# Stacking a stick-breaking head's operands three jobs ahead, and filler that runs on into the second group's values

## The chip, the cores and the metric

The kernel runs on one core of one Trainium2 chip. A core has five engines that work side by side, each through its own queue in order: TensorE (PE in the profile, its weight loads PEld) multiplies matrices, VectorE (DVE) and ScalarE (ACT) work element by element, GpSimd (POOL) does the same from on-chip memory only, and SyncE (SP) issues the DMAs. The metric is the time of one execution on the device in microseconds (us), given as the median of several runs.

## What is computed

One layer of a decoder on 512 tokens of width 2048, in float32, with two groups of attention heads side by side:

```python
h = rmsnorm(x, ln_mix)
sb_q, sb_k, sb_v, sw_q, sw_k, sw_v = split(h @ w_in)       # 16 x 64 (three times), 16 x 64, 4 x 64, 4 x 64
# group A, 16 heads, stick-breaking, strictly causal:
z = (sb_q * 64 ** -0.5) @ sb_k.T
log_beta, log_one_minus = log_sigmoid(z), where(causal, log_sigmoid(-z), 0)
survive = reversed_cumsum(log_one_minus) - log_one_minus
out_a = where(causal, exp(log_beta + survive), 0) @ sb_v
# group B, 16 query heads on 4 key heads: window of 128, ALiBi slopes, learned sinks
out_b = softmax_with_sink(sw_q, sw_k, sw_v)
x = x + concat(rmsnorm(out_a), rmsnorm(out_b)) @ w_out
gate, up = split(rmsnorm(x) @ w_gate_up)
x = x + (silu(gate) * up) @ w_down
return rmsnorm(x)
```

## The kernel before

Every float32 operand of a matmul is split into a high part and a rest in a faster float format, and a product is made of three matmuls (high by high, high by rest, rest by high). So each slab of weights that a DMA brings (`raw`) is split once, by ACT (`whi`, L215) and DVE (`wlo`, L216).

**Filler.** The projections lie in a list, `queue`, of slabs; a slab is a list of steps of three matmuls. `step()` issues the next step, and with a slab's third step it loads the slabs behind and splits the next. `pull(ns, mark)` adds `ns` to a running budget, `carry`, and issues steps until the budget is used up or the slab `mark` is reached; a step takes 648 off the budget, or 324 for a step of the second group's values. A budget that can't be spent stays in `carry` for the next `pull`. `drain(mark)` issues all steps up to a mark without touching the budget. In the part that the change touches the list holds, in this order: for each of eight pairs of stick-breaking heads four slabs of eight steps (`add_qk`; L408, L409, L410), four slabs of eight steps for the second group's keys (up to `sb_mark`), and four slabs of sixteen steps for its values (`add_swv`; L376, L377, L378; up to `swv_end`). A pair's projection collects in two banks of on-chip accumulator memory; the last steps of each half end in `q_evac` (L683) or `k_evac` (L686), which scale it on DVE into the tile `qk`. The next pair uses the same two banks.

**The stick-breaking loop.** A job is one block of one head: block 2 (two short key blocks together), block 1, block 0, so 48 jobs for 16 heads. `sb_begin(h)` drains the projection of head h's pair and stacks its operands: the high part of q twice over each other and its rest likewise (`stack_two`: ACT L692, DVE L693, L694, L695), and the high part of k over its rest (`stack_one`: ACT L701, DVE L702), on 64 rows each, so that two matmuls make the scores. `q1`, `q2` and `ks` have two buffers each. One turn j of the loop takes several jobs a stage further:

- `sb_log` (job j): absolute value, exponential, logarithm on ACT (L859 to L861)
- `sb_qk` (job j + 1): the score matmuls (L846, L847) into a bank `z`
- `sb_sum` (job j - 1): the cumulative sums as matmuls (L904) onto the same bank; `sb_w`: exponential and its high part on ACT (L918, L919)
- `sb_sp` (job j): DVE (L866), high part on ACT (L867); `sb_acc`: running sums on POOL (L884 to L894)
- `sb_av` (job j - 2): the output matmuls (L934) and, after a head's block 0, the sum of two halves on ACT and DVE (L706, L708)
- `sb_wsplit` (job j - 1; DVE L924), `sb_lo` (job j; DVE L872), `sb_mask` (job j + 1; DVE L852)

Three times a turn, between these stages, `pull(SBFILL / 3, sb_mark)` adds filler: 3381 a turn, 5.2 steps. The loop runs two turns past the last job. Behind it `drain(sb_mark)` and a `pull` of 16000 issue what is left up to the last slab of the values.

**What follows.** The sliding-window group uses the same list as filler, with a budget of its own per job; ahead of its first scores (L1061) stands `pull(2600.0)`. Its operands `kst` and `qst` are stacked by the same helpers (L692 to L702) into buffers that held the stick-breaking values, and `swv`, the values' tile, takes the buffer of `kq`, from which `qst` is stacked.

The program is written in one order; a scheduler draws up each engine's own order from it, by readiness as it estimates it and by place in the program, except where an instruction is kept in program order.

Of the kernel before, what the change touches and what calls it, by code (L numbers as in the profile page):

```python
# [37 lines left out]
def tile_hymba(ctx: ExitStack, tc: tile.TileContext, x, ln_mix, w_in, sb_norm, swa_norm,  # L38
# [183 lines left out]
    def step():  # L222

        i, m = pos
        sl = queue[i]
        if m == 0:
            split(i)
            if sl["pre"]:
                sl["pre"]()
        if m == min(2, len(sl["mms"]) - 1):  # L230
            for k in (1, 2):
                if i + k < len(queue):
                    load(i + k)
            if i + 1 < len(queue):
                split(i + 1)
        t = sl["mms"][m](sl["hi"], sl["lo"])
        pos[1] += 1
        if pos[1] == len(sl["mms"]):
            pos[0] += 1
            pos[1] = 0  # L240
            if sl["post"]:
                sl["post"]()
        for d in list(due):
            d[0] -= 1
            if d[0] <= 0:
                due.remove(d)
                d[1]()
        return t

    def pull(ns, mark=None):  # L250

        mark = len(queue) if mark is None else mark
        carry[0] += ns
        while carry[0] > 0 and pos[0] < mark:
            carry[0] -= step()
# [4 lines left out]
    def drain(mark=None):  # L260

        mark = len(queue) if mark is None else mark
        while pos[0] < mark:
            step()
# [423 lines left out]
    def stack_two(src, r0, hi, lo):  # L688

        s64 = src[r0:r0 + HD]  # L690
        r1 = HD - r0
        A.activation(out=hi[r0:r0 + HD], in_=s64, func=AF.Copy)  # L692
        V.tensor_copy(out=hi[r1:r1 + HD], in_=s64)  # L693
        V.tensor_tensor(out=lo[r0:r0 + HD], in0=s64, in1=f(hi)[r0:r0 + HD], op=ALU.subtract)  # L694
        V.tensor_copy(out=lo[r1:r1 + HD], in_=f(lo)[r0:r0 + HD])  # L695

    def stack_one(src, r0, st):

        s64 = src[r0:r0 + HD]
        r1 = HD - r0  # L700
        A.activation(out=st[r0:r0 + HD], in_=s64, func=AF.Copy)  # L701
        V.tensor_tensor(out=st[r1:r1 + HD], in0=s64, in1=f(st)[r0:r0 + HD], op=ALU.subtract)  # L702
# [38 lines left out]
    def sbt(dt, name, n=512, bufs=1):  # L741
        return phase[1].tile([P, n], dt, tag=name, name=name, bufs=bufs)
# [65 lines left out]
    sb_mark = len(queue)  # L808
    add_swv()
    swv_end = len(queue)  # L810
# [10 lines left out]
    def sb_begin(h):  # L821
        drain(marks[h // 2])
        H = Head()
        heads[h] = H
        H.r0 = (h % 2) * HD
        qk = qks[h // 2]
        H.q1, H.q2, H.ks = sbt(F32R, "q1", bufs=2), sbt(F32R, "q2", bufs=2), sbt(F32R, "ks", bufs=2)
        stack_two(qk[:, 0, :], H.r0, H.q1, H.q2)
        stack_one(qk[:, 1, :], H.r0, H.ks)
        H.acc = [None] * 3  # L830
        H.blk = [None] * 3
# [110 lines left out]
    jobs = [(h, i) for h in range(16) for i in (2, 1, 0)]  # L942
    NJ = len(jobs)

    def at(fn, j):
        if 0 <= j < NJ:
            fn(*jobs[j])

    SBFILL = SB_SLABS * 8 * 648.0 / 46
# [2 lines left out]
    at(sb_qk, 0)  # L952
    at(sb_mask, 0)
    for j in range(NJ + 2):
        if j + 2 < NJ and jobs[j + 2][1] == 2:
            sb_begin(jobs[j + 2][0])
        at(sb_log, j)
        at(sb_qk, j + 1)
        pull(SBFILL / 3, sb_mark)
        at(sb_sum, j - 1)  # L960
        at(sb_w, j - 1)
        at(sb_sp, j)
        at(sb_acc, j)
        pull(SBFILL / 3, sb_mark)
        at(sb_av, j - 2)
        at(sb_wsplit, j - 1)
        at(sb_lo, j)
        at(sb_mask, j + 1)
        pull(SBFILL / 3, sb_mark)
    drain(sb_mark)  # L970
    pull(16000.0, swv_end - 1)


    swp = open_phase("swp", 15)
# [161 lines left out]
    jobs = [(g, blk) for g in range(4) for blk in range(NT)]  # L1136
    NJ = len(jobs)
# [715 lines left out]
```

## Time and profile before

| what | us |
|---|---|
| three runs | 2018.45 median, 2017.85 to 2019.76 |
| the profiled execution's own time | 2018.88 |
| its span, from the first instruction to the last | 2017.2 |
| PE busy | 1989.7 |
| ACT busy | 1512.6 |
| DVE busy | 1478.7 |
| POOL busy | 1121.8 |
| score matmuls of the stick-breaking loop, first to last start | 162.6 to 419.9 |

A row of a group names the line, the engine, the operation, out<-in by tile, the shape, the count, the busy time and the mean duration in ns, then the engine's idle time just before and what ended it. A row of waits names who waited, for whom, the total in us, how often, and the longest. A row of the timeline begins with start and duration in us. A busy PE is not PE at its peak, since the ends of matmuls are modelled; between full-rate matmuls of 512 columns the timeline has 0.23 us from start to start.

### The profile page before, as it was taken

The numbers are of one execution on the slowest core, as the hardware profiler recorded it, in microseconds if no ns is written. First come the engines' busy times: TensorE is split into PE (matmuls) and PEld (weight loads), VectorE is DVE, ScalarE is ACT, GpSimd is POOL, SyncE is SP. The second block draws the span as 40 slices with busy tenths as digits, with TensorE's granted clock in tenths as the row PEclk, the third lists the DMA queues.
The fourth block names the chain that finished last, engine by engine and source line by source line (L and its number), as shares of the span: only waits on it lengthen the run. The fifth ranks groups of instructions, "written<-read, shape, count | busy, mean of one in ns | idle before, by whom it ended". The sixth has DMA issues, their size and how long they took to land.

```text
span 2017.2 us, 29170 instructions
## 1 busy us (share of the span) xinstructions
PE 1989.7 (99%) x10268; PEld 1697.7 (84%) x10268; DVE 1478.7 (73%) x1972; ACT 1512.6 (75%) x2031; POOL 1121.8 (56%) x599
## 2 busy tenths in 40 slices
PE   9999999999999999999999999999999999999998
PEld 8888777788888888888888888888888888888886
DVE  6677777767984777777777777777777867767767
ACT  6766777766773478777777777777777788788787
POOL 2833445430010066766667666666766778878883
PEclk9999999999999999999999999999999999999999
DMA  6412222122233354453544535444353643533523
GB/s 205 140 57 80 63 60 62 60 71 74 94 126 121 117 166 119 117 139 101 138 113 123 133 103 142 109 127 130 106 141 106 265 157 111 178 129 107 174 86 115
DMA packets 283298, 240.23 MB, mean 119 GB/s; under 512 B 11024, under 2 KB 233296, under 8 KB 280720
## 3 DMA queue, kind: packets, MB, share of 16 engines
q1 hardware_dynamic: 281392, 231.52, 38.6%
q0 software_dynamic: 1376, 5.52, 0.8%
q8 instruction: 81, 1.33, 0.3%
q10 hardware_dynamic: 384, 1.34, 0.2%
q14 instruction: 65, 0.53, 0.1%
HBM read 218.40 MB, written 19.92 MB: 118 GB/s over the span
## 4 chain that ended last, share of the span: by engine, by line
PE 89%; DVE 5%; ACT 4%; issue 2%; DMA 0%; DVEq 0%; ACTq 0%; POOL 0%; POOLq 0%
PE o L118 36%; PE m L118 30%; PE m L408 2%; PE m L410 2%; PE m L409 2%; PE m L376 2%; PE m L378 1%; PE m L377 1%; PE z L118 1%; PE o L377 1%; PE o L376 1%; PE o L378 1%; PE z L904 1%; DVE l L872 1%; ACT e L918 1%
## 5 line engine op out<-in xcount | busy, mean ns | idle before, releaser
L118 POOL TENSOR_TENSOR t<-raw,t 128x1024 f32<-128x1024 f32 x111 | 282.3, 2543 | 281.3 <-ACT hp L118 263.5
L118 DVE TENSOR_TENSOR wlo<-t,hp 128x1024 fp32r<-128x1024 f32 x247 | 301.2, 1219 | 184.3 <-PE o L118 112.9
L118 ACT ACTIVATE whi<-t 128x1024 fp32r<-128x1024 f32 x247 | 262.2, 1061 | 126.2 <-PE o L118 76.4
L118 POOL TENSOR_TENSOR t<-raw,raw 128x1024 f32<-128x1024 f32 x114 | 295.2, 2593 | 22.4 <-issue 11.3
L118 PE MATMUL o<-hca,whi 128*128 128x512 f32 x880 | 307.5, 391 | 0.0
L118 DVE TENSOR_TENSOR wlo<-raw,hp 128x1024 fp32r<-128x1024 f32 x187 | 228.2, 1221 | 92.1 <-issue 51.7
L118 ACT ACTIVATE whi<-raw 128x1024 fp32r<-128x1024 f32 (+1 forms) x189 | 200.0, 1058 | 105.0 <-PE m L118 74.8
L118 ACT ACTIVATE hp<-t 128x1024 fp32r<-128x1024 f32 x247 | 249.1, 1009 | 2.6 <-POOL t L118 2.6
L118 PE MATMUL o<-hca,wlo 128*128 128x256 f32 x880 | 244.0, 280 | 0.0
L118 ACT ACTIVATE hp<-raw 128x1024 fp32r<-128x1024 f32 x191 | 192.9, 1010 | 3.0 <-DMA raw<-in_w_down_dram 2.0
L118 PEld LDWEIGHTS o<-hca,whi 128*128 128x128 f32 x880 | 164.2, 187 | 35.8
L118 PE MATMUL m<-hca,whi 128*128 128x512 f32 x528 | 186.3, 392 | 1.1 <-DVE hca L118 1.1
L118 PEld LDWEIGHTS o<-hca,wlo 128*128 128x128 f32 x880 | 165.6, 189 | 0.4
L216 DVE TENSOR_TENSOR wlo<-raw,whi 128x1024 fp32r<-128x1024 f32 x87 | 110.4, 1269 | 65.0 <-ACT whi L215 64.5
L215 ACT ACTIVATE whi<-raw 128x1024 fp32r<-128x1024 f32 x87 | 91.8, 1055 | 78.4 <-PE o L378 32.4
L118 PE MATMUL m<-whi,dca 128*128 128x512 f32 x592 | 146.9, 389 | 0.0
L118 PE MATMUL o<-whi,dca 128*128 128x512 f32 x592 | 146.9, 389 | 0.0
L118 PE MATMUL m<-hca,wlo 128*128 128x256 f32 x528 | 146.3, 280 | 0.0
L118 PEld LDWEIGHTS o<-whi,dca 128*128 128x128 f32 x592 | 111.0, 188 | 23.2
L118 PEld LDWEIGHTS m<-whi,dca 128*128 128x128 f32 x592 | 111.0, 188 | 23.0
L408 PE MATMUL m<-hhi,whi 128*128 128x512 f32 x320 | 126.8, 396 | 2.2 <-DVE qk L686 2.1
L118 PE MATMUL m<-hcs,whi 128*128 128x512 f32 x352 | 125.9, 392 | 0.0
(371 smaller groups left out, 5233.6 us busy)
## 6 DMA issues: line engine op xcount, KB each, us to landing
raw<-in_w_gate_up_dram SPq DMA_DIRECT2D x348, 256.0 KB, 5.2
raw<-in_w_down_dram SPq DMA_DIRECT2D x68, 512.0 KB, 4.9
raw<-in_w_in_dram SPq DMA_DIRECT2D x35, 512.0 KB, 3.7
raw<-in_w_in_dram SPq DMA_DIRECT2D x66, 256.0 KB, 3.3
raw<-in_w_out_dram SPq DMA_DIRECT2D x32, 512.0 KB, 3.7
aT<-w SPq DMA_DIRECT2D x44, 256.0 KB, 3.5
xd<-aT SPq DMA_DIRECT2D x10, 1024.0 KB, 7.3
rx<-in_w_down_dram SPq DMA_DIRECT2D x20, 512.0 KB, 5.9
```

The costliest lines, as they stand in the source:

```text
L118: return lambda *a, **k: tc.keep_in_program_order(fn(*a, **k))
L215: A.activation(out=hi, in_=raw, func=AF.Copy)
L216: V.tensor_tensor(out=lo, in0=raw, in1=f(hi), op=ALU.subtract)
L376: mm(o, lhsT=lh[:, sl], rhs=hi[:, j, :], start=first, stop=False, skip_group_check=halves)
L377: mm(o, lhsT=lh[:, sl], rhs=lo[:, j, :], start=False, stop=False, skip_group_check=halves)
L378: mm(o, lhsT=ll[:, sl], rhs=hi[:, j, :], start=False, stop=(k == nslab * a - 1), skip_group_check=halves)
L408: mm(o, lhsT=wh, rhs=xh, start=(k == 0), stop=False)
L409: mm(o, lhsT=wh, rhs=xl, start=False, stop=False)
L410: mm(o, lhsT=wl, rhs=xh, start=False, stop=(k == KT - 1))
L872: V.tensor_tensor(out=B.l[:, a:w], in0=B.e, in1=f(B.h)[:, a:w], op=ALU.subtract)
L904: mm(zb[:, o:o + r.shape[1]], lhsT=lhsT, rhs=r, start=False, stop=last, skip_group_check=True)
L918: A.activation(out=B.e, in_=B.z, func=AF.Exp)
```

## The change

Two things, both in the stick-breaking loop. `sb_begin` of the next head (and in it the drain of that head's pair) is issued three jobs ahead, which is in the turn of the running head's block 2, where it was two jobs ahead, in the turn of block 1. And the three pulls in the loop may run on through the second group's values up to the last of their slabs, where they stopped at `sb_mark`; the pull behind the loop gets a budget of 6000 in place of 16000.

```diff
     for j in range(NJ + 2):
-        if j + 2 < NJ and jobs[j + 2][1] == 2:
-            sb_begin(jobs[j + 2][0])
+        if j + 3 < NJ and jobs[j + 3][1] == 2:
+            sb_begin(jobs[j + 3][0])
         at(sb_log, j)
         at(sb_qk, j + 1)
-        pull(SBFILL / 3, sb_mark)
+        pull(SBFILL / 3, swv_end - 1)
         at(sb_sum, j - 1)
         at(sb_w, j - 1)
         at(sb_sp, j)
         at(sb_acc, j)
-        pull(SBFILL / 3, sb_mark)
+        pull(SBFILL / 3, swv_end - 1)
         at(sb_av, j - 2)
         at(sb_wsplit, j - 1)
         at(sb_lo, j)
         at(sb_mask, j + 1)
-        pull(SBFILL / 3, sb_mark)
+        pull(SBFILL / 3, swv_end - 1)
     drain(sb_mark)
-    pull(16000.0, swv_end - 1)
+    pull(6000.0, swv_end - 1)
```

## The prediction

> **What bounds the kernel now.** I read the page first, then the busy time by stretches, then TensorE's waits in the stretches that are not full, then the timeline around the longest wait.
>
> ```profile
> span 2017.2 us, 29170 instructions
> PE 1989.7 (99%) x10268; PEld 1697.7 (84%) x10268; DVE 1478.7 (73%) x1972; ACT 1512.6 (75%) x2031; POOL 1121.8 (56%) x599
> ```
>
> TensorE (PE) is the bound. No matmul is added or dropped, so the change can move only time in which PE stands still or runs at a lower clock: 2017.2 - 1989.7 = 27.5 us, plus the clock. The stretches say where; the columns are the stretch, its length, then busy time and count of PE, weight loads, VectorE (DVE), ScalarE (ACT) and GpSimd (POOL), the granted clock, the DMA share and GB/s.
>
> ```profile
> 160.00:213.00 53.00, 53.00 (x258) 45.02 (x257) 37.73 (x60) 39.00 (x72) 21.03 (x32) 1.00 0.24 70
> 200.00:240.00 40.00, 37.62 (x173) 31.20 (x173) 29.40 (x45) 30.29 (x56) 18.07 (x24) 0.96 0.21 60
> 320.00:360.00 40.00, 35.81 (x165) 28.41 (x164) 31.20 (x48) 30.43 (x55) 21.03 (x26) 1.00 0.19 53
> 400.00:424.00 24.00, 22.49 (x108) 18.38 (x107) 16.05 (x26) 18.75 (x34) 14.27 (x20) 1.00 0.21 67
> 424.00:452.00 28.00, 26.25 (x203) 24.86 (x202) 20.62 (x31) 17.27 (x29) 6.11 (x7) 1.00 0.24 76
> 730.00:2000.00 1270.00, 1268.60 (x6737) 1094.28 (x6737) 935.25 (x1046) 1013.84 (x1109) 883.92 (x361) 1.00 0.45 130
> ```
>
> From 730 us on PE is full, and the first 53 us of the stick-breaking loop are full too. The holes lie between 213 and 436 us, inside that loop. PE's waits from 200 to 400 us, then from 400 to 445 us (total, times, longest):
>
> ```profile
> PE z L846 <- DVE ks L702: 6.9, 5, 2.2
> PE m L408 <- DVE qk L686: 2.1, 4, 1.6
> PE o L934 <- DVE l L924: 0.5, 2, 0.3
> ...
> PE o L934 <- ACT h L919: 2.3, 2, 1.6
> PE o L934 <- DVE l L924: 1.0, 3, 0.4
> ```
>
> Together 12.8 us. The largest is what the change names: the score matmuls of a new head (L846) wait for the last operand that is stacked (L702). The timeline of the longest, DVE first, then PE:
>
> ```profile
> 215.68 0.42 DVE L693 CAST q<-qk 64x512 fp32r<-64x512 f32 x1
> 217.30 0.56 DVE L866 SCALAR_TENSOR_TENSOR e<-z,e 128x384 f32<-128x384 f32 x1 [1.20 <-ACT e L861]
> 217.77 0.68 DVE L924 TENSOR_TENSOR l<-e,h 128x512 fp32r<-128x512 f32 x1
> 218.37 1.23 DVE L694 TENSOR_TENSOR q<-qk,q 64x512 fp32r<-64x512 f32 x1
> 219.53 0.63 DVE L872 TENSOR_TENSOR l<-e,h 128x384 fp32r<-128x384 f32 x1
> 220.09 0.67 DVE L686 TENSOR_TENSOR qk<-m,rbc 128x512 f32<-128x512 f32 x1
> 220.80 0.67 DVE L695 CAST q<-q 64x512 fp32r<-64x512 f32 x1
> 221.50 1.64 DVE L216 TENSOR_TENSOR wlo<-raw,whi 128x1024 fp32r<-128x1024 f32 x1
> 223.17 0.68 DVE L702 TENSOR_TENSOR ks<-qk,ks 64x512 fp32r<-64x512 f32 x1
> ...
> 220.82 0.50 PE L408 MATMUL m<-hhi,whi 128*128 128x512 f32 x1 [0.17 <-DVE qk L686]
> 221.39 0.40 PE L410 MATMUL m<-hhi,wlo 128*128 128x512 f32 x1
> 224.00 0.35 PE L846 MATMUL z<-q,ks 128*128 128x256 f32 x1 [2.21 <-DVE ks L702]
> ```
>
> DVE works almost without a pause from 217.30 to 223.85: evacuation (L686), stacking (L693 to L695, L702), the running head's chain (L866, L924, L872) and a filler split (L216) share these 6.5 us, and the next head's scores come due in the middle. The wait has an after-effect on the clock:
>
> ```profile
> 220.00:225.00 5.00, 2.62 (x12) 0.99 0.10 30
> 225.00:230.00 5.00, 5.00 (x20) 0.67 0.26 76
> ```
>
> At a granted clock of 0.67 the second stretch loses 5 x 0.33 = 1.65 us, with the first (5 x 0.01) **1.7 us**. The clock is 1.00 in the other stretches shown, so the shorter waits did not do this. The Trainium skill ("TensorE: Matmul & The Clock Gate", Part 1) has the clock fall back only after an idle window of about 3.4 us; the trace does not agree, since 2.21 us preceded a fall here. By the page's rule this term would be nil and the forecast below about 1.7 us later.
>
> **The change, part by part.** One job (one of three blocks of one head) takes 5.5 us: 47 jobs lie between the first and last start of this row.
>
> ```profile
> L846 PE MATMUL z<-q,ks x64: 277/333/393, 162.6 to 419.9; 128*128 128x256 f32 x32, 128*128 128x384 f32 x16, 128*128 128x512 f32 x16
> ```
>
> *Stacking three jobs ahead.* All 15 stackings in the loop, with the drain ahead of each, move up one job, past one round of filler and chain on ACT and DVE; no DMA is issued other than those of the filler steps, in their order on SP. The buffers (two of each operand) are free in time: those of head h - 2 are read last in the score matmuls issued two jobs earlier. The operands gain about 5.5 us on their use, and the longest lateness is 2.2 us. So the five waits go: **-6.9 us**, and with them the clock stretch: **-1.7 us** (bounds 0 and the whole for both).
>
> Every head pair's projection must be drained one job earlier. Counting the steps in the code (648 each against 3381 a job, 5.2 steps), the drain before head 2 grows from 4 steps to 10; the later ones stay at 0 or 1. Ten steps of 0.68 us (three matmuls 0.23 us apart) are work that PE does anyway. What could stop it there is the next slab's split; in 131 to 154 us filler ran alone and PE was full:
>
> ```profile
> 131.00:154.00 23.00, 23.00 (x105) 18.75 (x104) 16.23 (x27) 12.37 (x20) 0.35 (x2) 1.00 0.41 118
> ```
>
> So 0, at worst one late split, 1.6 us (L216 above).
>
> What is late next: the next pair's filler still needs the two banks that L683 and L686 empty. Those 2.1 us stay as they are: 0, between -2.1 (a less crowded job) and +2.1 (as much again).
>
> The stacking now falls into the job that runs block 2, ahead of its L866, L924 and L872 on DVE. Those feed L904 and L934 one and two jobs later. The trace shows what displaced chain steps cost now: 0.5 us in 200 to 400 us. I take 1.0 us more, **+1.0**; the bounds are 0 and 15 stackings at 0.4 us, the longest such wait, 6 us. I stay near the low end because at the old place the crowd is larger: there it also meets the head's output sum (L708, below), and the new job has none.
>
> *Filler into the second group's values.* Before, the projection steps end in job 45 by the same count; jobs 46 to 49 have no filler of their own, and 48 value steps follow behind the loop. Now jobs 45 to 49 take 9, 10, 11, 10 and 8 of them.
>
> ```profile
> L376 PE MATMUL m<-whi,hhi x64: 278/283/386, 423.8 to 452.0; 128*128 128x256 f32 x64
> L376 PE MATMUL m<-whi,hhi x44: 280/283/386, 436.3 to 452.0; 128*128 128x256 f32 x44
> L934 PE MATMUL o<-l,vst x64: 274/337/502, 175.4 to 435.8; 128*128 128x256 f32 x32, 128*128 128x384 f32 x16, 128*128 128x512 f32 x16
> L1061 PE MATMUL z<-kst,qst x64: 277/283/283, 463.9 to 593.3; 128*128 128x256 f32 x64
> L702 DVE TENSOR_TENSOR qst<-kq,qst x8: 676/686/690, 430.3 to 439.1; 64x512 fp32r<-64x512 f32 x8
> L686 DVE TENSOR_TENSOR kq<-m,rbc x2: 674/676/679, 418.9 to 423.3; 128x512 f32<-128x512 f32 x2
> L708 DVE TENSOR_TENSOR oA<-o,oc x3: 683/684/684, 411.8 to 437.8; 64x512 f32<-64x512 f32 x3
> ```
>
> Of 64 value steps (one L376 each, the first row) 44 run after the last output matmul (started at 435.8), only 20 beside the waiting chain; the L934 waits there are 3.3 us. With a full ration each job resembles those of 200 to 400 us. I take **-2.5 us** (0 to -3.3), not all, because the stacking for the second group (L702, 430.3 to 439.1) stays on DVE. A seam is added: the value steps need the banks that L686 empties at 418.9 and 423.3. At 2.1 us over seven such seams that is **+0.3** (0 to 1.6, the longest).
>
> The time behind the loop gets shorter. Now 27.6 us of pure filler lie between the end of the last output matmul (435.8 + 0.5) and the first window scores (463.9). After the change the budget gives 16 value steps (15.7/44 = 0.36 us each) and 7 projection steps (0.68): 10.5 us. The scores need stacks that end by 440 us, 4 us after the last output matmul, so it suffices. Later waits of that phase may shift; the longest I found there in the whole trace is
>
> ```profile
> PE z L1112 <- DVE s L1104: 2.4, 2, 1.5
> ```
>
> so **+0.5** (-2.4 to +1.5).
>
> **Sum**: -6.9 - 1.7 + 1.0 - 2.5 + 0.3 + 0.5 = **-9.3 us**. The profiled execution took 2018.88 us, 1.7 more than its span; 2018.88 - 9.3 = 2009.6. The median shown is 2018.45, 0.4 lower: **2009.2 us**.
>
> **The rivals.** *The wait only moves.* DVE does the same work, and what it does earlier delays something else: the banks (L408) or the outputs (L934) take back the 6.9 us. For it: DVE is busy 29 to 31 of 40 us here. Against: in 160 to 213 us, with the same work per job, DVE was busy 37.7 of 53 us and no wait came up, so a job's delay can be worked off in the next. Then 2018.45 - 1.7 - 2.5 + 0.8 = **2015.0**.
>
> *It doesn't do what it says.* The order on each engine is drawn up from the program by a scheduler; 20 value steps already run ahead of their place in the program. If it puts the stacking where it was, the waits stay: **2018**.
>
> *Slower: the stacking in front of the chain.* A head's four DVE pieces (L693 0.42 and L702 0.68, L694 and L695 at the same, as their shapes are the same: 2.2 us) stand together ahead of L866 and L924. Between the end of L924 (218.45) and its reader L934 (219.36) lie
>
> ```profile
> 219.36 0.39 PE L934 MATMUL o<-h,vst 128*128 128x512 f32 x1
> ```
>
> 0.9 us, so 1.3 us per head, 15 heads, 20 us: 2018.45 - 6.9 - 1.7 - 2.5 + 0.8 + 20 = **2028**. It decides from (6.9 + 1.7 + 2.5 - 0.8)/15 = 0.7 us a head. Against it: these pieces stood in the chain's way in the other job too, where L934 lost 0.5 us in all. The Trainium skill (the same page, on engine queue depths) has ACT and DVE work strictly first in, first out, which is this rival's condition.
>
> *Everything goes*, bank waits and tail included: 2018.45 - 6.9 - 1.7 - 3.3 - 2.1 = **2004.4**.
>
> **How the numbers follow.** Forecast 0.60, wait moves 0.14, no effect 0.10, slower 0.08, everything 0.08. A measurement tells 0.2%, 4 us, from no change: faster means under 2014.4. The forecast (but for 0.02), all of "everything" and 0.05 of "moves" lie there: 0.71. The rest of "moves", the forecast's 0.02 and nearly all of "no effect" make 0.20, the slower rival and 0.01 from "no effect" 0.09. The range of 8 in 10 runs from 2005.0, the forecast without the rest of the tail (0.8), the displaced chain (1.0), the two seams (0.8) and most of the bank waits (1.6), to 2017.0, 2 us past the moved wait; it leaves out the slower rival, most of "no effect" and half of "everything".
>
> **What would show it.** In the profile after, L846 <- L702 should be gone or under 0.5 us, the clock 1.00 from 160 to 440 us, L934's waits behind 400 us under 1 us, and L376 should start about five jobs before the last L934 with about 20 of its steps, not 44, behind it. L408 <- L686 should stand near 2 us. I am wrong if L934 or L904 waits grow past 5 us inside the loop, if L1061's first start waits for a stack, or if the stacking's place on DVE is unchanged.

## The result, and the profile after

The changed kernel takes 2003.18 us (median of four runs, 2002.74 to 2003.48), the kernel before 2018.51 on the same chip: a ratio of 0.9924 with a 95% interval of 0.9912 to 0.9936, 15.3 us less. The forecast was 2009.2 with a range from 2005.0 to 2017.0, so the direction was right and the gain is 6 us larger than forecast, outside the range. The profiled execution of the changed kernel took 2003.03 us, against 2018.88.

From the page after:

```profile
span 2000.9 us, 29118 instructions
PE 1983.5 (99%) x10268; PEld 1697.5 (85%) x10268; DVE 1479.4 (74%) x1972; ACT 1512.2 (76%) x2031; POOL 1115.7 (56%) x599
```

The same counts on the five engines, 16.3 us less span. PE's busy time fell by 6.2 us with the same matmuls; that is the first sign that "busy" had hidden a loss. The stretches, with the columns as before:

```profile
160.00:213.00 53.00, 53.00 (x255) 44.82 (x254) 38.98 (x60) 38.30 (x69) 20.86 (x30) 1.00 0.27 79
200.00:240.00 40.00, 40.00 (x194) 33.95 (x193) 29.67 (x47) 32.20 (x59) 20.98 (x30) 1.00 0.23 67
320.00:360.00 40.00, 39.29 (x193) 33.06 (x192) 32.46 (x51) 32.86 (x61) 18.66 (x26) 1.00 0.20 60
400.00:424.00 24.00, 24.00 (x166) 22.53 (x165) 16.83 (x27) 20.41 (x36) 9.24 (x13) 1.00 0.21 67
424.00:452.00 28.00, 26.41 (x168) 23.97 (x167) 20.36 (x44) 14.65 (x30) 2.40 (x4) 1.00 0.25 76
```

The holes of 200 to 240 and 400 to 424 us are closed, the one of 320 to 360 us has shrunk from 4.2 to 0.7 us, and the granted clock stays at 1.00. PE's waits after, from 200 to 400 us and then from 400 to 445 us:

```profile
PE o L934 <- DVE l L924: 2.6, 4, 1.2
PE m L408 <- DVE qk L683: 0.7, 2, 0.4
...
PE m L376 <- DVE swv L268: 1.6, 1, 1.6
```

L846 no longer waits for a stacking. The waits at the outputs (L934) inside the loop are five times what they were, and there is a new one: the last slab of the value steps waits for the evacuation of its own bank.

Of the signs that the prediction named, one failed plainly: the waits for L686 did not stay near 2 us, they are gone, and 0.7 us for L683 stand there. L376 starts at 408.0 us, four jobs and not five before the last L934, and 17 of its steps lie behind that.

Shown waits fell from 12.8 to 4.9 us, 7.9 us; the span fell by twice that. To find the rest I added up, over the trace's matmuls, the time from one start to the next less 0.2268 us per 512 columns (the pace of the timeline's undisturbed 512-column matmuls). This sum is the **loss**. "Loop" is from the first L846 to the last head's first L846, "tail" on to the last L934, "seam" on to the first window scores (L1061), "window" on to the last matmul of that phase (L1126). In us:

| kernel | loop | tail | seam | window |
|---|---|---|---|---|
| before | 18.7 | 6.0 | 1.2 | 12.7 |
| the change | 8.5 | 1.1 | 2.1 | 10.7 |
| difference | -10.2 | -5.0 | +0.9 | -2.1 |

That is -16.4 us, the span's difference to 0.1. In loop and tail before, 24.7 us were lost where the wait list shows 12.9. Not all of it is waiting: 4.0 us are delays of under 0.02 us each, of which the changed kernel has as many (4.6 us), and 1.6 us are the stretch at half clock. The other 19.1 us stand against the 12.9 shown. One reason can be seen in single rows: a matmul's row is 0.39 us long but the next may start 0.23 after it, so a matmul that is late by up to 0.16 us shows no wait at all, and every shown wait is 0.16 us too short. In the kernel before:

```profile
220.27 0.39 PE L410 MATMUL m<-hhi,wlo 128*128 128x512 f32 x1
```

The next matmul started at 220.82 (in the prediction), 0.55 us later: 0.32 us lost, 0.17 shown.

### The profile page after: what moved, and what is told of

It reads as the page before. It is cut to its first block, busy times and chain, and to the rows that moved or that the text cites. A ratio compares the mean times of both kernels' runs of the same rounds, so it can differ in the third digit from the quotient of the medians.

```text
span 2000.9 us, 29118 instructions
## 1 busy us (share of the span) xinstructions
PE 1983.5 (99%) x10268; PEld 1697.5 (85%) x10268; DVE 1479.4 (74%) x1972; ACT 1512.2 (76%) x2031; POOL 1115.7 (56%) x599
## 4 chain that ended last, share of the span: by engine, by line
PE 93%; DVE 3%; ACT 3%; issue 1%; DVEq 0%; POOL 0%; ACTq 0%; POOLq 0%
PE o L118 36%; PE m L118 30%; PE m L408 3%; PE m L409 3%; PE m L410 2%; PE m L376 2%; PE m L378 2%; PE m L377 2%; PE z L118 1%; PE o L378 1%; PE o L376 1%; PE o L377 1%; PE z L904 1%; PE o L934 1%; PE z L1112 1%
## 5 line engine op out<-in xcount | busy, mean ns | idle before, releaser
L118 POOL TENSOR_TENSOR t<-raw,t 128x1024 f32<-128x1024 f32 x111 | 282.3, 2543 | 281.1 <-ACT hp L118 262.8
L118 POOL TENSOR_TENSOR t<-raw,raw 128x1024 f32<-128x1024 f32 x114 | 294.7, 2588 | 23.5 <-issue 12.1
L216 DVE TENSOR_TENSOR wlo<-raw,whi 128x1024 fp32r<-128x1024 f32 x87 | 108.7, 1249 | 56.0 <-ACT whi L215 53.7
L408 PE MATMUL m<-hhi,whi 128*128 128x512 f32 x320 | 125.9, 393 | 0.7 <-DVE qk L683 0.7
```

The source lines that it names most:

```text
L118: return lambda *a, **k: tc.keep_in_program_order(fn(*a, **k))
L216: V.tensor_tensor(out=lo, in0=raw, in1=f(hi), op=ALU.subtract)
L408: mm(o, lhsT=wh, rhs=xh, start=(k == 0), stop=False)
```

## The experiments

All were timed beside the kernel before on the same chip (2018.1 to 2018.5 us). The loss is from each kernel's profiled execution. Some of these hold stretches of 3.4 us at half clock, up to 1.7 us of loss each: one in the seam of stack1, drain4_fill, sum_later and drain4_sum_later, one in the window phase of stack3_only, drain5_fill and drain5_sum_later, two in that of drain6_fill.

| kernel | us | ratio to before, 95% | loop | tail | seam | window |
|---|---|---|---|---|---|---|
| stack3_only | 2009.13 | 0.9957 (0.9944 to 0.9969) | 8.5 | 4.6 | 1.1 | 14.4 |
| fill_only | 2012.99 | 0.9975 (0.9965 to 0.9985) | 18.6 | 1.5 | 1.9 | 10.6 |
| post6000_only | 2017.22 | 0.9994 (0.9985 to 1.0004) | 18.6 | 6.0 | 1.2 | 11.0 |
| drain3_stack2 | 2007.21 | 0.9951 (0.9938 to 0.9963) | 7.1 | 5.3 | 1.1 | 12.5 |
| drain3_fill | 2003.34 | 0.9920 (0.9908 to 0.9933) | 7.1 | 1.1 | 2.7 | 10.6 |
| stack1 | 2003.78 | 0.9925 (0.9911 to 0.9938) | 7.1 | 1.1 | 4.0 | 10.8 |
| drain4_fill | 2013.44 | 0.9973 (0.9962 to 0.9984) | 16.1 | 3.9 | 1.6 | 11.1 |
| stack4 | 2016.89 | 0.9991 (0.9981 to 1.0000) | 20.0 | 3.9 | 0.3 | 12.4 |
| drain5_fill | 2022.28 | 1.0019 (1.0010 to 1.0028) | 19.9 | 4.7 | 0.1 | 17.4 |
| drain6_fill | 2015.32 | 0.9983 (0.9974 to 0.9992) | 6.5 | 2.5 | 0.1 | 23.5 |
| split5 | 2003.58 | 0.9923 (0.9911 to 0.9936) | 9.1 | 1.1 | 2.1 | 10.6 |
| drain4_split5 | 2013.22 | 0.9973 (0.9963 to 0.9984) | 16.7 | 3.9 | 0.3 | 12.5 |
| sum_later | 2006.68 | 0.9942 (0.9928 to 0.9957) | 10.2 | 1.1 | 4.4 | 10.7 |
| drain5_sum_later | 2021.92 | 1.0019 (1.0009 to 1.0029) | 19.9 | 4.7 | 0.1 | 16.0 |
| drain4_sum_later | 2012.04 | 0.9968 (0.9957 to 0.9980) | 15.5 | 3.9 | 1.8 | 10.9 |

### The two parts of the change, one by one

stack3_only, the kernel before with

```diff
-        if j + 2 < NJ and jobs[j + 2][1] == 2:
-            sb_begin(jobs[j + 2][0])
+        if j + 3 < NJ and jobs[j + 3][1] == 2:
+            sb_begin(jobs[j + 3][0])
```

> The kernel before with the stacking and its drain three jobs ahead, and the pulls as they were. Theory A (the change is two parts that add up; a wait of PE costs what the starts of its matmuls lose, more than the idle time shown): L846 <- L702 is gone (-8.5 us from start to start), the half clock is gone (-1.6), the bank waits L408 <- L686 fall by some 3, L934's waits in the loop grow by about 2.5, and the tail behind 410 us keeps its 3 us of waits: 2018.5 - 10.6 = 2008. Rival B (the gain of 15.3 us is the stacking's alone, the filler part is worth nothing): 2003 to 2004. Rival C (the parts need each other, since both move the same filler): 2014 or more.

fill_only, the kernel before with the other lines:

```diff
-        pull(SBFILL / 3, sb_mark)
+        pull(SBFILL / 3, swv_end - 1)
...
-    pull(16000.0, swv_end - 1)
+    pull(6000.0, swv_end - 1)
```

> The kernel before with the pulls of the change (filler into the values inside the loop, 6000 behind it) and the stacking two jobs ahead. Theory A: the tail's waits go (-4), one wait for the values' evacuation comes (+1.8), the window phase gains 2: 2018.5 - 4.5 = 2014. The five L846 waits and the half clock stay. Rival B: 2018 to 2019. Rival C: 2016 to 2018, with tail waits left over 2 us.

post6000_only, the last line alone:

> The kernel before with only the budget behind the loop cut from 16000 to 6000. By the count of steps the same 48 value steps are issued there (the unspent budget of jobs 46 to 49 is 13000), but 10000 less is carried into the window phase. Theory A: if the window phase's 2 us come from the lower budget, L1112's waits fall from 2.4 to under 0.5 us and the time is 2016 to 2017. Rival: they come from where the values run, and the time is 2018 to 2019 with L1112's waits as before.

The parts gain 9.2 and 5.4 us, 14.6 together, where the change gains 15.3: they add up, each within 1.2 us of theory A, and rivals B and C are out. The loss table says which part acts where: the stacking's part takes the loop from 18.7 to 8.5 us and leaves 4.6 us of the tail; the filler's part leaves the loop at 18.6 and takes the tail to 1.5. In the wait list of fill_only, from 200 to 445 us, the loop's old waits stand all but untouched:

```profile
PE z L846 <- DVE ks L702: 6.9, 5, 2.2
PE m L408 <- DVE qk L686: 1.8, 2, 1.6
PE o L934 <- DVE l L924: 0.6, 2, 0.3
```

The lower budget alone takes the window phase from 12.7 to 11.0 us, with L1112's waits down from 2.4 to 0.2 us as its theory A said. Its time lies 1.1 us lower; that is inside the interval, so of the time alone it can't be told.

post6000_only answers a second question, by chance. Its first long wait is as long as in the kernel before, but no stretch at half clock follows it, and then the next head's wait is there, which the kernel before did not have at that place:

```profile
224.14 0.35 PE L846 MATMUL z<-q,ks 128*128 128x256 f32 x1 [2.22 <-DVE ks L702]
257.33 0.36 PE L846 MATMUL z<-q,ks 128*128 128x256 f32 x1 [1.32 <-DVE ks L702]
```

With the fall of the clock the loop before lost 8.5 us at L846 and L847 and 1.6 in the slow stretch; without it 9.7 and nothing. That fits ACT and DVE catching up during the slow stretch, so that 1.2 of its 1.6 us come back at the next wait; over the whole loop the loss is 18.7 us with the fall and 18.6 without.

### Is it the lead of the stacking?

Three kernels separate the drain of a pair's projection from the stacking. drain3_stack2 is the kernel before with the drain alone three jobs ahead:

```diff
+        if j + 3 < NJ and jobs[j + 3][1] == 2:
+            drain(marks[jobs[j + 3][0] // 2])
         if j + 2 < NJ and jobs[j + 2][1] == 2:
             sb_begin(jobs[j + 2][0])
```

> The kernel before with the drain of a pair's projection three jobs ahead, but the stacking itself left two jobs ahead, pulls as they were. Theory P (what counts is that the projection ends earlier, so that its evacuation and the stacking don't fall into one job): L846 waits under 1 us, bank waits as in stack3_only, time within 1.5 us of it, 2007 to 2009.5. Rival S (what counts is the stacking's own place in the program, which puts its instructions ahead of others on DVE): L846 waits of 4 us and more stay, 2012 or more.

drain3_fill is the same with the filler into the values; stack1 has the stacking one job ahead, in the turn that reads it:

```diff
+        if j + 3 < NJ and jobs[j + 3][1] == 2:
+            drain(marks[jobs[j + 3][0] // 2])
-        if j + 3 < NJ and jobs[j + 3][1] == 2:
-            sb_begin(jobs[j + 3][0])
+        if j + 1 < NJ and jobs[j + 1][1] == 2:
+            sb_begin(jobs[j + 1][0])
```

> The changed kernel with the stacking put back to two jobs ahead, its drain left three ahead (with the filler into the values). Theory A (the loop, the tail and the window phase add up, and the drain's place is what the loop gains by): no L846 wait, loop losses as in drain3_stack2 (1.4 us less than the change), the rest as in the change: 2003.2 - 1.4 = 2001.8, between 2001 and 2003.5. Rival S (the stacking's place in the program matters once the tail is full too): 2005 or more.

> The changed kernel with the drain three jobs ahead, but the stacking one job ahead, in the turn whose score matmuls read it. It measures the price of a wait. Theory A: the L846 waits are back where a stacking isn't ready; with n such waits of W us together by the wait list, the time is that of drain3_fill plus W + 0.2 to 0.25 n (what the overlap of matmul ends hides), whatever the granted clock shows. Rival C (the clock's falls add their own 1.7 us each): time over that sum by 1.7 for each stretch at half clock. If the scheduler starts the stackings early by itself (their inputs are ready), W is under 2 us and the time as drain3_fill.

The stacking's own place in the program shows nothing in the time: with it three, two or one job ahead that is 2003.2, 2003.3 and 2003.8 us. stack1 has no L846 wait at all, so it could not measure the price of one. The traces show why. L686 for the pair of heads 4 and 5 starts at 220.1 us in the kernel before, and at 215.3 to 215.8 in the changed kernel and these three; head 4's last piece of stacking (L702) ends at 223.9 before, and at 218.2 to 219.1 in the four, wherever the program has the stacking. What the line `j + 3` moves is the end of the projection. That agrees with theory P, though drain3_stack2 lies 1.9 us below stack3_only where 1.5 was allowed: with the stacking two or one job ahead the loop loses 7.1 us, not 8.5. The 1.4 us forecast from this for drain3_fill didn't show in the median; 0.6 of them went to its last value slab, which waits 2.2 us in place of 1.6.

### Is it the lead of the drain?

drain4_fill, drain5_fill and drain6_fill have the drain four, five and six jobs ahead and the stacking two; stack4 has both four ahead. The edit of drain5_fill, against drain3_fill:

```diff
-        if j + 3 < NJ and jobs[j + 3][1] == 2:
-            drain(marks[jobs[j + 3][0] // 2])
+        if j + 5 < NJ and jobs[j + 5][1] == 2:
+            drain(marks[jobs[j + 5][0] // 2])
```

> The same with the drain four jobs ahead, in the turn that runs block 0, the stacking two ahead. Theory L (the lead counts: any turn early enough will do): no L846 wait, bank waits L408 of 1 us or less, 2001 to 2004. Rival T (the turn counts: the bank waits fell because the turn of block 2 has no output sum on DVE): bank waits of 2 us and more are back, with the losses they bring 2004 to 2007.

> The changed kernel with drain and stacking four jobs ahead (head 1 is stacked ahead of the loop). Theory A: there is no L846 wait left to win; the time stays within 2 us of the change, 2001.5 to 2005. Rival (the displaced chain, the slower case of the prediction: a stacking further ahead stands in front of more of the running head's work): L934 and L904 waits grow from 2.6 us to over 6, 2007 or more.

> The changed kernel with the drain five jobs ahead, which is the turn of block 1 again, as before the change, the stacking two ahead. Theory T (what costs is the turn in which a pair's projection ends, with the split of the next slabs tied to it; the lead counts only until the stacking is ready): no L846 wait, losses at L408 and L934 in the loop as in the kernel before (5 us from start to start, 1.8 more than drain3_fill), time 2003.5 to 2007. Rival L (the further ahead, the worse: 3 gives 2003.3, 4 gives 2013.4): 2014 or more.

> The same with the drain six jobs ahead, the turn of block 2, as in the change. Theory T: the loop's losses are those of drain3_fill (7 us in all, L934 2.6, L408 0.8); the filler ends 16 steps sooner, so some of the tail's waits come back: 2004 to 2008. Rival L: 2014 or more, with loop losses over 16 us.

No kernel of these has an L846 wait, and yet in two of the three turns the loop loses about as much as before the change (16.1 to 20.0 us against 18.7). Waits from 163 to 400 us in drain5_fill (the turn of block 1, as before the change), drain4_fill (block 0) and drain6_fill (block 2, as in the change):

```profile
PE o L934 <- DVE l L924: 7.4, 16, 1.1
PE m L408 <- DVE qk L683: 1.0, 2, 0.5
PE m L408 <- DVE qk L686: 0.7, 3, 0.4
```

```profile
PE o L934 <- DVE l L924: 5.5, 7, 1.5
PE m L408 <- DVE qk L686: 2.0, 5, 0.6
```

```profile
PE o L934 <- DVE l L924: 1.9, 3, 1.2
```

By turn, the loop's loss is 18.7 and 19.9 us (block 1: two and five ahead), 16.1 and 20.0 (block 0: drain4_fill, stack4), and 8.5, 7.1, 7.1, 7.1 and 6.5 (block 2: three and six ahead). The lead does not order them, the turn does. So theory T held for the loop, and rival L, which expected over 16 us there for six jobs ahead, is out. The times alone would not say so: 2022.3 us for drain5_fill and 2015.3 for drain6_fill both lie where rival L had them. Theory T's price for drain5_fill was too low by a factor of three: it expected 5 us at L408 and L934, and 15.8 were lost there. drain6_fill is slow for a reason of its own: its filler runs out sooner, and the window phase loses 23.5 us, of which the last value slab's wait for L268 alone is 5.2. drain4_fill and stack4 went against their first theories: bank waits of 2.0 us are back in the one, at a time 6 us past what rival T allowed, and L934 and L904 wait 8.4 us in the other.

What a wrong turn does can be read at drain5_fill's longest wait. First ACT, PE and DVE rows of one job, from the end of its sums to its output (other rows left out):

```profile
280.73 0.40 PE L904 MATMUL z<-l,negu 128*128 128x512 f32 x1
280.92 1.05 ACT L215 ACTIVATE whi<-raw 128x1024 fp32r<-128x1024 f32 x1
281.88 0.61 ACT L692 ACTIVATE q<-qk 64x512 fp32r<-64x512 f32 x1
283.42 0.62 ACT L701 ACTIVATE ks<-qk 64x512 fp32r<-64x512 f32 x1
284.46 0.47 ACT L918 ACTIVATE e<-z 128x384 f32<-128x384 f32 x1
285.44 0.51 ACT L919 ACTIVATE h<-e 128x384 fp32r<-128x384 f32 x1
287.40 0.55 DVE L924 TENSOR_TENSOR l<-e,h 128x384 fp32r<-128x384 f32 x1
288.00 0.39 PE L934 MATMUL o<-l,vst 128*128 128x256 f32 x1 [1.10 <-DVE l L924]
```

and what DVE did ahead of that L924:

```profile
284.59 1.11 DVE L694 TENSOR_TENSOR q<-qk,q 64x512 fp32r<-64x512 f32 x1
285.74 0.69 DVE L702 TENSOR_TENSOR ks<-qk,ks 64x512 fp32r<-64x512 f32 x1
286.35 0.41 DVE L695 CAST q<-q 64x512 fp32r<-64x512 f32 x1
286.79 0.69 DVE L866 SCALAR_TENSOR_TENSOR e<-z,e 128x512 f32<-128x512 f32 x1
```

The sums end at 281.1, the exponential (L918) starts 3.3 us later, behind a filler split and two pieces of stacking on ACT; its high part (L919) is done at 285.95, and L924 starts 1.4 us later, behind three pieces of stacking and L866 on DVE. In this job that is the prediction's slower rival, the stacking ahead of the chain, in another turn than the one it was feared for. In the changed kernel a job of block 0 runs like this (other rows left out), with no stacking in its way, and L924 ends 2.5 us before its reader:

```profile
296.94 0.39 PE L904 MATMUL z<-l,negu 128*128 128x512 f32 x1
299.22 0.58 ACT L918 ACTIVATE e<-z 128x512 f32<-128x512 f32 x1
299.83 0.63 ACT L919 ACTIVATE h<-e 128x512 fp32r<-128x512 f32 x1
300.50 0.69 DVE L924 TENSOR_TENSOR l<-e,h 128x512 fp32r<-128x512 f32 x1 [0.54 <-ACT h L919]
303.71 0.39 PE L934 MATMUL o<-l,vst 128*128 128x512 f32 x1
```

Over heads 2 to 13 the mean time from the last L904 of a job to its L918 is 2.7, 2.2 and 1.8 us for blocks 2, 1 and 0 in the changed kernel, and 3.5, 4.3 and 4.0 in drain5_fill.

But most jobs of drain5_fill are late without any stacking in the way. Of these 36 jobs 13 have a piece of it on ACT between their last L904 and L918, and L918 comes 3.5 us after on average; in the other 23 it comes 4.2 us after. What goes with the turn is the order of the jobs on ACT: the chain of the job two later (its L859) runs ahead of a job's L918 in 35 of the 36 in drain5_fill, 31 in the kernel before, 29 in drain4_fill and 28 in stack4, but in 22 in the changed kernel, 21 in drain3_fill and 25 in drain6_fill. L924 is done on average 0.45 us ahead of its output matmul in drain5_fill and 0.75 in drain4_fill, and 1.8, 2.0 and 2.2 us ahead in the last three.

### Why the turn matters: two tries that missed

split5 and drain4_split5 issue the split of the next filler slab later, since the waits that are left had an L216 ahead of L924:

```diff
-        if m == min(2, len(sl["mms"]) - 1):
+        if m == min(5 if 11 <= i < 43 else 2, len(sl["mms"]) - 1):
```

> The changed kernel with the split of the next filler slab (ACT L215, DVE L216) issued with a slab's sixth step instead of its third, for the slabs of the loop. Theory W (the waits L934 <- L924 that are left come from a split of 1.2 us that stands right ahead of L924 on DVE): L934's waits fall from 2.6 us to under 1, 2000.5 to 2002.5. Rival (the split comes late and the filler waits for it): PE waits for whi or wlo of 2 us and more, 2004 or more.

> drain4_fill with the split issued with a slab's sixth step. Theory W: L934's 8 us of waits fall to under 3, the time from 2013.4 to 2009 or less. Rival (they come from the stacking and evacuation in the turn of block 0, not from the split): L934's waits stay over 6 us, 2012 or more.

Theory W fell: the times are the same within the intervals, L934 waits 3.3 us in split5, more than the change's 2.6, and drain4_split5 came as its rival said.

The sum_later kernels issue a head's output sum one turn later:

```diff
         if i == 0:
-            o = oA[h // 8][:, (h % 8) // 2, :]
-            halves_added(H.ob, [(o[H.r0:H.r0 + HD], lambda a: a)], sbt(F32, "oc"))
...
+            sums.append(lambda: sb_out(h))
...
+        ready = list(sums)
+        sums.clear()
         at(sb_av, j - 2)
         at(sb_wsplit, j - 1)
         at(sb_lo, j)
+        for fn in ready:
+            fn()
```

> The changed kernel with the output sum of a head (ACT L706, DVE L708, ACT L713 or L715) issued one turn later, behind that turn's work for the chain. Theory O (the turn matters because of the output sum, which meets the evacuation and the stacking): the sum now falls into the turn of block 0, away from the drain's turn and the one behind it; L934's waits fall from 2.6 to under 1.5 us, 2001 to 2003.5. Rival (the sum is small beside the rest): 2002.5 to 2004.5, waits as before.

> drain5_fill (drain in the turn of block 1) with the output sum one turn later. Theory O: the loop's loss at L934 falls from 12 us to under 5 and the time from 2022.3 to 2015 or less. Rival (another thing that is tied to the turn, such as where the filler slabs and their splits begin): L934 still loses 9 us and more, 2019 or more.

> drain4_fill (drain in the turn of block 0) with the output sum one turn later, which is the drain's own turn. Theory O: worse, L934's loss over 9 us, 2014 or more. Rival: within 1.5 us of drain4_fill's 2013.4.

Theory O fell as well: with the sum moved, the loop's loss stays at 19.9 us in the turn of block 1 and is 15.5 in place of 16.1 in that of block 0. The changed kernel gets slower by 3.5 us, past both ranges of sum_later: 1.7 us of that are lost in the loop, the rest at the seam, with the stretch at half clock. That the output sum stands in the turn of block 1, on which the prediction leaned, is not why that turn is bad. Why the block-2 turn is the good one stays open: the order that the scheduler draws up changes as a whole with the drain's turn, and no run here held that order fixed, so that the order on ACT is the cause is not shown either. No kernel beat the changed one by more than its interval.

## Why the forecast was off, step by step

| step of the forecast | forecast | measured loss |
|---|---|---|
| L846's waits go, and the half clock | -6.9 - 1.7 | -8.5 - 1.6 |
| bank waits (L408 <- L686) stay | 0 | -2.9 |
| chain displaced in the loop (L934) | +1.0 | +2.7 |
| tail filled with value steps | -2.5 | -5.0 |
| seam to the values and to the window phase | +0.3 | +0.9 |
| window phase | +0.5 | -2.1 |

**Where the time would come from** was right: the whole difference lies between 163 and 617 us, and PE was the bound throughout.

**The step that failed first is the price of a wait.** The sum took the wait list's idle time as the cost. In the loop and tail 12.9 us of shown idle stood for 19.1 us of late starts, so the terms made of it were too small: the 6.9 us at L846 were worth 8.5, and the tail, taken at 2.5 with 3.3 as its bound, gave 5.0. From this alone the bound "everything goes" of 2004.4 was no bound, and the range stopped short of the result.

**"Those 2.1 us stay as they are"** was the second. From the end of a pair's projection to its L686, DVE took 2.1 to 5.6 us for the pairs of heads 4 to 15 before, and takes 0.8 to 3.6 now; the loss at L408 and L409 fell from 4.2 to 1.2 us. The sum had no reason to hold DVE's delay fixed when the drain moved to another turn; the lower bound it named, -2.1, was the better value, and by the loss it was -2.9.

**The window phase** was given the wrong sign. post6000_only shows most of it in the budget: with 10000 less carried in, the phase loses 11.0 in place of 12.7 us.

**The reason given for the largest term was not enough, its size nearly right.** "The operands gain about 5.5 us on their use" is true, and the L846 waits went with every longer lead. But drain5_fill gives the operands more time still and its loop loses 19.9 us against 18.7 before: there the rival "the wait only moves" came true, from L846 to L934. That the time was kept comes from the turn into which the drain fell, and that three jobs ahead is such a turn was luck: the one argument for it, the crowd (L708 in the old turn), pointed the right way for a reason that drain5_sum_later refutes.

**The displaced chain** was sized at +1.0 and measured +2.7, inside its bounds of 0 to 6; as the slower rival, its mechanism is seen in the longest wait of drain5_fill, but most late jobs there have no stacking ahead of them. **The clock** term should not stand beside the waits: by the comparison with post6000_only, some 1.2 of the 1.6 us of the slow stretch came back at the next wait.

**The seam** came at another place than named: not the banks that L686 empties, but the evacuation of the last value slab (L267 on ACT, L268 on DVE). In the changed kernel:

```profile
433.32 0.63 ACT L715 ACTIVATE oc<-oA 128x512 f32<-128x512 f32 x1 [2.23 <-DVE oA L708]
433.98 0.47 ACT L267 ACTIVATE swv<-m,rstd 128x256 fp32r<-128x256 f32 x1
```

L267 stands behind L715 on ACT, and L715 waits for the last head's output sum (L708), which DVE ran at 432.60, behind the last stackings for the second group (L702, to 432.23). These L702 are also the last readers of `kq`, whose buffer `swv` takes over; in drain6_fill L267 itself waits for them, 1.86 us. A buffer of its own for `swv` was not tried.

## What to carry to other kernels

Price a wait by the starts of the instructions on the bound engine, against their undisturbed pace, and not by the idle time that a wait list shows: here the list had 12.9 us where 19.1 were lost. When a step is moved ahead to take a wait away, vary the distance past the one that was meant: if a longer lead brings the loss back at another line, the gain hangs on where the step and its companions landed, and not on the lead alone. And split a change into its parts with a table of loss by stage; parts that add up, as here, can then be tuned one at a time.

## What the runs showed of the hardware

The same wait of PE does not always bring the clock down: 2.21 us before L846 were followed by 3.4 us at half clock in the kernel before, 2.22 us at the same place in post6000_only by none. At the seam, 2.19 us ahead of L376 brought it down in stack1 and not in drain3_fill. In the slow stretch of the kernel before, matmuls of 512 columns start 0.43 us apart in place of 0.23. The Trainium skill ("TensorE: Matmul & The Clock Gate", Part 1) describes windows of about 3.4 us that run freely and are not set off by the program; the length of the slow stretch agrees (3.41 us), and that the outcome differs from one execution to another fits a window whose place is not tied to the wait. What it says of a whole idle window before a fall does not agree with the 2.21 us here.
